# Two encoder layers on one core: normalised x of the experts split straight from x, modulation weights in units of one contraction tile

## The chip, the cores and the metric

The kernel runs on one core of a Trainium2 chip. The metric is the device time of one execution in microseconds (us), from a run without the profiler; below it is the median of three such runs. Two further numbers belong to one profiled execution: its own time, and its span, from its first instruction to its last.

## The reference

Two layers are computed on 256 tokens of width 1024. Each has a mixer half and an expert half, and each half scales and shifts its normalised input by a modulation that comes from a condition vector `c`:

```python
cond = silu(c)
for l in range(2):
    sh1, sc1, gt1, sh2, sc2, gt2 = split(cond @ w_ada[l] + b_ada[l], 6)   # w_ada[l]: 1024 x 6144
    h = rms_norm(x, g_norm1[l]) * (1 + sc1) + sh1
    x = x + gt1 * hybrid_mixer(h, ...)          # input projection, three attentions, gates, output projection
    h = rms_norm(x, g_norm2[l]) * (1 + sc2) + sh2
    x = x + gt2 * hier_moe(h, ...)              # router: best of 4 groups, best 2 of its 8 experts; SwiGLU
```

All arrays are float32. `cond @ w_ada` is a product of one row with a large matrix: 1024 rows are contracted, in eight tiles of 128 (the contraction tiles below).

## The kernel before

**Order.** The order of the instructions is written out by hand: what the program calls first stands first on its engine, and each engine works off its own list in order. A layer is a generator `mixer(l)` followed by `moe(l)`.

**Mixer.** `mixer` makes a list of 94 jobs: the input projection in 18 chunks of 384 columns (four jobs each), the two small projections of the latent attention, and the branch and output projections. A job has a first half, which splits a weight piece on ScalarE and VectorE into two rounded parts (lines 591 to 605), and a second half of matmuls on TensorE (607 to 622). The loop at lines 1380 to 1407 issues the first halves some four jobs ahead of the second halves, puts pieces of attention work between the jobs, and at chosen jobs one step of the modulation generator (`next(bg)`, 1406).

**Modulation.** `ada(l, g)` (386 to 421) computes one third of a layer's modulation row: g = 0 for the mixer's scale and shift, 1 for the experts', 2 for the two gates. A third has 2048 columns, in four blocks of 512. The condition vector's slice is the stationary operand, broadcast over 32 columns, so that block j goes to rows 32j to 32j+31 of one accumulator: four blocks use four separate 32-column groups of the array. A third's weights, 16384 columns of 128 rows, come contraction tile by contraction tile (2048 columns each), but are loaded in units of 3072 columns: five of 1.5 MB and one of 0.5 MB. A step takes one unit and issues its matmuls, six in each of the first five and two in the last; two more steps add the bias and transpose the row into columns. Layer 0's own first third is done by `ada_half` (423) in a layout of its own.

**Loads.** Weights come through the SP queue in one fixed order, `self.stream`, which `plan` (191) builds from `schedule` (152): the chunks in the order of their use, three jobs ahead, and the modulation units at the steps where they are due. `pump` (73) issues the next loads of that order while fewer than `self.ring` units are held, and is called whenever a buffer is given back. In the mixer `ring` is 3; the buffers are 12 of 1.5 MB (`u`), shared with the mixer's large intermediates. `early(l)` is 2 in layer 1: two modulation steps of its experts' third are done before the job loop, beside the normalisation of x (1307).

**Head of the experts.** `moe` (1412) transposes x into `x2T`, takes 1/rms from sums of squares that are there already, and writes the normalised x, `xn` (line 506, VectorE). TensorE computes the router's logits, `lg` (1426), and puts x into the result's accumulators, `y` (1431). ScalarE rounds xn to `xhi` (1441); GpSimd subtracts to get the rest, `xlo` (1442). VectorE picks groups and experts from the logits (1437 to 1486). TensorE sums the choices to ranks, `rk` (1488), then spreads the gate rows, `gth` (line 459, called at 1493). VectorE makes the positions `R` (1501) and the one-hot matrices `Poh` (1557), with which TensorE gathers the tokens, `ga` (1575); ScalarE copies them out as `xT` (1582), and the first expert's matmuls `A` start (1621). 32 experts follow, each with three 1.5 MB units, except that the third units of experts 0 and 1 come as 0.5 MB pieces (`load_pieces`).

Of the kernel before, what the change touches and what calls it, by code (L numbers as in the profile page):

```python
# [7 lines left out]
F32R = mybir.dt.float32r  # L8
BF = mybir.dt.bfloat16
I32 = mybir.dt.int32  # L10
AF = mybir.ActivationFunctionType
ALU = mybir.AluOpType
# [4 lines left out]
EPS = 1e-6  # L17
# [20 lines left out]
class Kern:  # L38
# [113 lines left out]
    def schedule(self, l):  # L152

        keys = []
        for c in range(10):
            keys += [('in', l, c)] * 4
            if c == 4:
                keys += [('uq', l)] * 4
            if c == 5:
                keys += [('ukv', l)] * 2  # L160
        first = len(keys)
        for c in range(10, 18):
            keys += [('in', l, c)] * 4
        last = len(keys)

        keys += [('bo', l, u) for u in [r // 3 for r in range(6)] + [2, 3, 3, 3] + [r // 3 for r in range(10, 18)]]
        if l == 0:
            keys[:12] = [keys[i] for i in self.FIRST]
        ada = [('ada', l, 1, u) for u in range(6)] + [('ada', l, 2, u) for u in range(6)]
        if l + 1 < self.layers:  # L170
            ada += [('ada', l + 1, 0, u) for u in range(6)]
        at = {}
        steps = []
        for k in ada:
            steps.append(k)
            if k[3] == 5:
                steps += [None, None]
        steps = steps[self.early(l):]
        lo, hi = 14 if l == 0 else 8, last - 5
        for n, k in enumerate(steps):  # L180
            at.setdefault(lo + n * (hi - lo) // len(steps), []).append(k)
        return keys, at
# [8 lines left out]
    def plan(self):  # L191
        a = self.a

        def src(k):
            if k[:3] == ('ada', 0, 0):
                c0 = k[3] // 3 * 8192 + k[3] % 3 * 3072
                return a['w_ada'][0, 0][:, c0:min(c0 + 3072, k[3] // 3 * 8192 + 8192)]
            if k[0] == 'ada':
                return a['w_ada'][k[1], k[2]][:, k[3] * 3072:min((k[3] + 1) * 3072, 16384)]
            if k[0] == 'in':  # L200
                return a['w_in'][k[1], k[2]]
            if k[0] in ('uq', 'ukv'):
                return a['w_' + k[0]][k[1]]
            if k[0] == 'bo':
                return a['w_bo'][k[1], k[2]]
            return a['w_e'][k[1], k[2]][:, k[3] * 3072:(k[3] + 1) * 3072]

        order = [('ada', 0, 0, u) for u in range(6)] + self.cut
        for l in range(self.layers):
            keys, at = self.schedule(l)  # L210
            seen = 0
            if l:
                order += [keys[0]] + [('ada', l, 1, u) for u in range(self.early(l))]
            for i in range(len(keys)):
                while seen < min(len(keys), i + 1 + self.AHEAD):
                    if keys[seen] not in order[-60:]:
                        order.append(keys[seen])
                    seen += 1
                order += [k for k in at.get(i, []) if k]
            order += [('e', l, e, u) for e in range(NE) for u in range(3) if ('e', l, e, u) not in self.beside(l)]  # L220
        s = [(k, src(k), 0) for k in order]
        first = [(k, x[:, i:i + 1536], i) for i in (0, 1536) for k, x, _ in s[6:9]]
        self.stream = deque(s[:3] + first[:3] + s[3:6] + first[3:] + s[9:])
        self.pieces = {}
# [161 lines left out]
    def ada(self, l, g):  # L386

        nc = self.nc
        ps = self.bank('ada')
        p = 0  # L390
        for u in range(6):
            key = ('ada', l, g, u)
            w = self.take(key)
            for i in range(6 if u < 5 else 2):
                kt, j = divmod(p, 4)
                self.mm(ps[32 * j:32 * j + 32], self.cond[:, kt:kt + 1].to_broadcast([128, 32]), w[:, i * 512:(i + 1) * 512], kt == 0, kt == 7)
                p += 1
            self.done(key)
            if u == 3:
                bz = self.load_bias(l, g)  # L400
            yield
        row = self.cp.tile([128, 512], F32, name=f"modrow_{l}", tag='modrow') if g == 2 else self.alloc('s', [128, 512], F32, 'modrow')
        nc.vector.tensor_add(row, ps, bz)
        self.free(ps, bz)
# [72 lines left out]
    def squares(self, ss, t, j, src=None):  # L477

        junk = self.alloc('s', [128, 512], F32, 'junk')
        self.nc.scalar.activation(junk, self.x[t][:, 512 * j:512 * j + 512] if src is None else src, AF.Square, scale=1.0 / 32,  # L480
                                  accum_out=ss[:, 2 * j + t:2 * j + t + 1])
        self.free(junk)

    def norm_x(self, name, ss=None, fill=None):

# [926 lines left out]
    def moe(self, l):  # L1412
        nc, tc = self.nc, self.tc
        ab = self.mod[l, 1]
        V = nc.vector
# [2 lines left out]
        self.router_row(l)  # L1418
        self.transposed(lambda t, k: self.x[t][:, 512 + k * 128:640 + k * 128], 4, None, None, full=xT[1:])
        self.router_row_all()  # L1420
        xn, rs = self.norm_x('xn2', self.ss)

        pt = self.bank('lg')
        for t in range(2):
            for kt in range(8):
                self.mm(pt[:, t * 64:t * 64 + 36], xT[kt // 4][:, kt % 4, t * 128:t * 128 + 128], self.wrs[:, kt], kt == 0, kt == 7)
        self.free(*xT)
        y = [[self.bank('y') for _ in range(2)] for _ in range(2)]
        for j in range(2):
            for t in range(2):  # L1430
                self.mm(y[t][j], self.ident, self.x[t][:, 512 * j:512 * j + 512], True, False)
        self.free(*self.x)
        xhi, xlo = ([self.alloc('w', [128, 1024], F32R, 'xp') for _ in range(2)] for _ in range(2))
        L = self.alloc('s', [128, 512], F32, 'L')
        lg = L[:, 0:72].rearrange("p (t n) -> p t n", t=2)
        for t in range(2):
            V.scalar_tensor_tensor(lg[:, t], pt[:, t * 64:t * 64 + 36], rs[:, t:t + 1], self.rrow,
                                   op0=ALU.mult, op1=ALU.add)
        self.free(pt)
        for t in range(2):  # L1440
            nc.scalar.activation(xhi[t], xn[t], AF.Copy)
            nc.gpsimd.tensor_sub(xlo[t], xn[t], xhi[t])
        self.free(*xn)
        self.load_pieces(l, 2)
        if l + 1 < self.layers:
            self.load_kr(l + 1)
            self.load_wr(l + 1)
# [42 lines left out]
        self.mm(pr[:, 32:64], self.tri[:, 0:128], Mb[:, 1], False, True)  # L1490
        self.mm(pr[:, 64:96], self.tri[:, 128:256], Mb[:, 0], True, False)
        self.mm(pr[:, 64:96], self.tri[:, 128:256], Mb[:, 1], False, True)
        gt = self.gate_halves(l)
        V.tensor_add(Mf, oh1, oh2)
        eg, gs, r2, sm = tmp(4), tmp(1), tmp(1), tmp(1)
        V.tensor_sub(eg, lgr, bc(gm, 4))
# [1 line left out]
        nc.scalar.activation(eg, eg, AF.Exp)  # L1498
        nc.scalar.activation(r2, r2, AF.Exp)
        nc.scalar.preload_act_table_set(SILU)  # L1500
        V.scalar_tensor_tensor(R, Mf, -4096.0, pr[:, 0:64].rearrange("p (t n) -> p t n", t=2), op0=ALU.mult, op1=ALU.add)

        def gates_and_blocks():
# [472 lines left out]
```

## Time and profile before

| | |
|---|---|
| median of three runs | 1390.2 us (1389.4 to 1391.21) |
| profiled execution, own time | 1390.37 us |
| its span | 1388.6 us |
| TensorE (PE) busy | 1329.2 us, 96% |
| VectorE (DVE), ScalarE (ACT), GpSimd (POOL) busy | 668.2, 538.4, 135.2 us |
| mean DMA rate over the span | 314 GB/s |
| mixer of layer 0, its experts | from the start to 347 us, to 715 us |
| mixer of layer 1, its experts | to 1017 us, to the end |

PE stands for matmuls and PEld for the loads of their stationary operand. A view in order of time gives start, duration, engine, line, operation, output and inputs, with the count of merged instructions (x12) and, in brackets, how long the engine had been idle before and what ended it. The matmul helper is line 102 for all callers, so the output's name tells which matmul it is.

### The profile page before, as it was taken

The numbers are of one execution on the slowest core, as the hardware profiler recorded it, in microseconds if no ns is written. First come the engines' busy times: TensorE is split into PE (matmuls) and PEld (weight loads), VectorE is DVE, ScalarE is ACT, GpSimd is POOL, SyncE is SP. The second block draws the span as 40 slices with busy tenths as digits, with TensorE's granted clock in tenths as the row PEclk, the third lists the DMA queues.
The fourth block names the chain that finished last, engine by engine and source line by source line (L and its number), as shares of the span: only waits on it lengthen the run. The fifth ranks groups of instructions, "written<-read, shape, count | busy, mean of one in ns | idle before, by whom it ended". The sixth has DMA issues, their size and how long they took to land. (4 is left out here: it accounts for less than half of the span.)

```text
span 1388.6 us, 19465 instructions
## 1 busy us (share of the span) xinstructions
PE 1329.2 (96%) x7666; PEld 869.3 (63%) x7666; DVE 668.2 (48%) x1417; ACT 538.4 (39%) x1140; POOL 135.2 (10%) x138
## 2 busy tenths in 40 slices
PE   5999999999899999999899999999999999999997
PEld 3788787887544444444358897888764444444443
DVE  5587564676623223332256775556762233323222
ACT  4554554574322222221155565447532222222211
POOL 0002064300100000000000202641010000000000
PEclk9999999999999999999999999999989999999999
DMA  9965457369589999999993626525858999999993
GB/s 373 374 246 222 184 204 289 129 246 360 222 345 425 425 425 424 425 426 425 420 421 151 227 91 232 191 94 202 358 214 318 404 425 425 425 424 427 424 424 147
DMA packets 45215, 437.95 MB, mean 315 GB/s; under 512 B 5080, under 2 KB 5608, under 8 KB 11328
## 3 DMA queue, kind: packets, MB, share of 16 engines
q1 hardware_dynamic: 44832, 435.78, 77.2%
q8 instruction: 62, 1.02, 0.3%
q0 software_dynamic: 288, 0.89, 0.2%
q14 instruction: 33, 0.27, 0.1%
HBM read 435.59 MB, written 1.05 MB: 314 GB/s over the span
## 5 line engine op out<-in xcount | busy, mean ns | idle before, releaser
L102 PE MATMUL in<-h,hH 128*128 128x384 f32 (+1 forms) x576 | 206.1, 358 | 3.7 <-ACT hH L1345 2.5
L1693 DVE TENSOR_TENSOR O<-O,gth 64x512 f32<-64x512 f32 (+1 forms) x132 | 88.8, 673 | 243.2 <-PE O L102 242.2
L102 PE MATMUL in<-h,hL 128*128 128x384 f32 (+1 forms) x576 | 195.3, 339 | 0.1
L102 PE MATMUL in<-l,hH 128*128 128x384 f32 (+1 forms) x576 | 194.5, 338 | 0.0
L1632 ACT ACTIVATE u<-A 64x384 f32<-64x384 f32 x64 | 31.1, 487 | 300.9 <-PE A L102 300.9
L102 PEld LDWEIGHTS in<-h,hH 128*128 128x128 f32 x576 | 109.0, 189 | 29.3 <-issue 17.1
L102 PEld LDWEIGHTS in<-h,hL 128*128 128x128 f32 x576 | 108.8, 189 | 1.4 <-DVE hL L1346 1.4
L102 PEld LDWEIGHTS in<-l,hH 128*128 128x128 f32 x576 | 109.2, 190 | 0.5
L1582 ACT ACTIVATE xT<-ga,modab 128x128 f32<-128x128 f32 x256 | 93.0, 468 | 20.6 <-PE ga L102 20.6
L1699 ACT ACTIVATE Op<-O 128x1024 fp32r<-128x1024 f32 x30 | 31.7, 1057 | 138.6 <-DVE O L1693 138.6
L1633 DVE SCALAR_TENSOR_TENSOR u<-A,m,u 64x384 f32<-64x384 f32 x64 | 39.4, 616 | 89.5 <-ACT u L1632 86.1
L102 PE MATMUL ga<-Poh,xp 128*128 128x256 f32 x512 | 71.4, 294 | 0.0
L102 PE MATMUL y<-Op,PTp 128*128 128x512 f32 x240 | 70.1, 415 | 0.0
L102 PEld LDWEIGHTS ga<-Poh,xp 128*128 128x128 f32 x512 | 65.8, 198 | 5.4 <-issue 4.0
L1602 DVE CAST PTp<-PTe 128x256 fp32r<-128x256 bf16 x32 | 13.6, 425 | 115.3 <-PE PTe L102 115.3
L803 POOL TENSOR_TENSOR rot<-TB,rope 128x256 f32<-128x256 f32 x8 | 11.7, 1487 | 488.6 <-ACT UC L873 429.3
L947 ACT ACTIVATE P<-P,m 128x256 f32<-128x256 f32 (+1 forms) x48 | 27.6, 576 | 79.2 <-DVE m L1005 37.1
L102 PEld LDWEIGHTS y<-Op,PTp 128*128 128x128 f32 x240 | 40.6, 188 | 21.0 <-issue 15.5
L1700 DVE TENSOR_TENSOR Op<-O,Op 128x1024 fp32r<-128x1024 f32 x30 | 36.8, 1225 | 33.8 <-ACT Op L1699 29.2
L1033 POOL TENSOR_SCALAR bias<-dist 128x128 f32<-128x128 f32 (+1 forms) x48 | 36.5, 761 | 5.2 <-PE oT L102 1.3
L1030 POOL TENSOR_SCALAR qz<-UC,gq 128x384 f32<-128x384 f32 x16 | 22.2, 1387 | 142.9 <-PE oT L102 72.7
L955 DVE TENSOR_SCALAR P<-P,m 128x256 f32<-128x256 f32 (+1 forms) x80 | 29.9, 407 | 1.8
(848 smaller groups left out, 2451.5 us busy)
## 6 DMA issues: line engine op xcount, KB each, us to landing
piece<-in_w_e SPq DMA_DIRECT2D x12, 512.0 KB, 6.8
w('ada', 0, 0, 0)_4_90<-in_w_ada SPq DMA_DIRECT2D x1, 1536.0 KB, 9.6
w('ada', 0, 0, 1)_5_92<-in_w_ada SPq DMA_DIRECT2D x1, 1536.0 KB
w('in', 0, 0)_9_104<-in_w_in SPq DMA_DIRECT2D x2, 768.0 KB, 16.5
w('in', 0, 1)_10_108<-in_w_in SPq DMA_DIRECT2D x2, 768.0 KB, 16.3
w('in', 0, 2)_11_110<-in_w_in SPq DMA_DIRECT2D x2, 768.0 KB, 12.2
w('ada', 0, 0, 3)_18_196<-in_w_ada SPq DMA_DIRECT2D x1, 1536.0 KB
w('ada', 0, 0, 4)_35_252<-in_w_ada SPq DMA_DIRECT2D x1, 1536.0 KB
```

The source lines that it names most:

```text
L102: self.nc.tensor.matmul(out, lhsT, rhs, start=start, stop=stop)
L947: nc.scalar.activation(dst, src, AF.Exp, bias=mx_neg[:, i:i + 1], scale=1.0, accum_out=sm[:, i:i + 1])
L955: nc.vector.tensor_scalar(dst, dst, r[:, i:i + 1], None, op0=ALU.mult)
L1030: nc.gpsimd.tensor_scalar(qz, M['qd'][:, pr::2, t * 128:t * 128 + 128], self.gq[:, l, 1 + hh:2 + hh], None, op0=ALU.mult)
L1033: nc.gpsimd.tensor_scalar(bias[:, lo:hi], self.dist[:, t, 256 + lo:256 + hi], -DIL_SLOPE[g][h], None, op0=ALU.mult)
L1582: nc.scalar.activation(dst, src, AF.Identity, scale=a2[:, kt:kt + 1], bias=s2[:, kt:kt + 1])
L1602: V.tensor_copy(PT[p], pv)
L1632: nc.scalar.activation(u[b:b + 64], A[c:c + 64, :384], AF.Silu)
L1633: V.scalar_tensor_tensor(u[b:b + 64], A[b:b + 64, :384], GC[e // 2][b:b + 64, e % 2:e % 2 + 1], u[b:b + 64], op0=ALU.mult, op1=ALU.mult)
L1693: V.tensor_mul(O[e // 2][b:b + 64, 512 * h + c:512 * h + c + n], o[c][p, :n], gt[p, c:c + n])
L1699: nc.scalar.activation(hi, whole, AF.Copy)
L1700: V.tensor_sub(lo, whole, hi)
```

## The change

Two parts. In the head of the experts, `xn` is no longer written: ScalarE makes `xhi` as the rounded x * (1/rms), with 1/rms as the per-row scale of its copy, and VectorE makes `xlo` as x * (1/rms) - xhi in one instruction. `low(0)` stands on VectorE ahead of the logits' first use, `low(1)` between the choice of the experts and the positions `R`. The gate rows (`gate_halves`) are issued right behind `y`, ahead of the ranks. The last two pieces are loaded after `low(1)`, and GpSimd's two loads for the next layer no longer stand behind its subtractions. In the modulation, a unit is one contraction tile: eight units of 2048 columns (1 MB) in place of six. A step takes two units and issues eight matmuls; a third has four such steps and two without weights. `early(l)` counts steps, so four units are taken early in layer 1, and the steps are spread anew over the same jobs.

```diff
-        for k in ada:
-            steps.append(k)
-            if k[3] == 5:
-                steps += [None, None]
+        for m, g in [(l, 1), (l, 2)] + [(l + 1, 0)] * (l + 1 < self.layers):
+            steps += [[('ada', m, g, u), ('ada', m, g, u + 1)] for u in range(0, 8, 2)] + [[], []]
         steps = steps[self.early(l):]
...
-                return a['w_ada'][k[1], k[2]][:, k[3] * 3072:min((k[3] + 1) * 3072, 16384)]
+                return a['w_ada'][k[1], k[2]][:, k[3] * 2048:(k[3] + 1) * 2048]
...
-        for u in range(6):
-            key = ('ada', l, g, u)
+        for kt in range(8):
+
+            key = ('ada', l, g, kt)
             w = self.take(key)
-            for i in range(6 if u < 5 else 2):
-                kt, j = divmod(p, 4)
-                self.mm(ps[32 * j:32 * j + 32], self.cond[:, kt:kt + 1].to_broadcast([128, 32]), w[:, i * 512:(i + 1) * 512], kt == 0, kt == 7)
-                p += 1
+            for j in range(4):
+                self.mm(ps[32 * j:32 * j + 32], self.cond[:, kt:kt + 1].to_broadcast([128, 32]), w[:, j * 512:(j + 1) * 512], kt == 0, kt == 7)
             self.done(key)
-            if u == 3:
+            if kt == 5:
                 bz = self.load_bias(l, g)
-            yield
+            if kt % 2:
+                yield
...
+    def norm_r(self, ss):
+        a = self.small(2)
+        self.nc.vector.scalar_tensor_tensor(a, ss[:, 0:2], EPS, ss[:, 2:4], op0=ALU.add, op1=ALU.add)
+        return self.rstd(a, 2)
...
-        xn, rs = self.norm_x('xn2', self.ss)
+        rs = self.norm_r(self.ss)
...
         self.free(*xT)
+
+        xhi, xlo = ([self.alloc('w', [128, 1024], F32R, 'xp') for _ in range(2)] for _ in range(2))
+        for t in range(2):
+            nc.scalar.activation(xhi[t], self.x[t], AF.Copy, scale=rs[:, t:t + 1])
+
+        def low(t):
+            V.scalar_tensor_tensor(xlo[t], self.x[t], rs[:, t:t + 1], xhi[t], op0=ALU.mult, op1=ALU.subtract)
+        low(0)
         y = [[self.bank('y') for _ in range(2)] for _ in range(2)]
         for j in range(2):
             for t in range(2):
                 self.mm(y[t][j], self.ident, self.x[t][:, 512 * j:512 * j + 512], True, False)
-        self.free(*self.x)
-        xhi, xlo = ([self.alloc('w', [128, 1024], F32R, 'xp') for _ in range(2)] for _ in range(2))
+        gt = self.gate_halves(l)
...
-        for t in range(2):
-            nc.scalar.activation(xhi[t], xn[t], AF.Copy)
-            nc.gpsimd.tensor_sub(xlo[t], xn[t], xhi[t])
-        self.free(*xn)
-        self.load_pieces(l, 2)
...
-        gt = self.gate_halves(l)
         V.tensor_add(Mf, oh1, oh2)
...
         nc.scalar.preload_act_table_set(SILU)
+        low(1)
+        self.free(*self.x)
+        self.load_pieces(l, 2)
         V.scalar_tensor_tensor(R, Mf, -4096.0, pr[:, 0:64].rearrange("p (t n) -> p t n", t=2), op0=ALU.mult, op1=ALU.add)
```

## Rows read from the trace of the kernel before

**Rows 1.** By stretch: length, busy PE PEld DVE ACT POOL, granted clock, DMA share, GB/s.

```profile
66.00:345.00 279.00, 276.54 (x1614) 226.03 (x1613) 185.39 (x388) 144.56 (x293) 61.51 (x62) 1.00 0.62 236
740.00:1015.00 275.00, 273.00 (x1584) 234.68 (x1583) 183.51 (x385) 149.83 (x311) 60.97 (x62) 1.00 0.51 197
...
365.00:369.00 4.00, 4.00 (x20) 3.63 (x20) 2.67 (x16) 3.68 (x9) 0.00 (x0) 0.56 0.02 6
```

**Rows 2.** Order of time, PE and PEld, around one modulation step of six matmuls.

```profile
740.06 0.33 PE L102 MATMUL in<-l,hH 128*128 128x384 f32 x1
...
740.24 0.34 PE L102 MATMUL in<-h,hL 128*128 128x384 f32 x1
...
740.50 1.91 PE L102 MATMUL ada<-ada', 1, 1, 2)_1137_5725,cond 128*32 128x512 f32 x12
740.96 0.12 PEld L102 LDWEIGHTS ada<-ada', 1, 1, 2)_1137_5725,cond 128*32 128x32 f32 x2 [0.30 <-issue]
741.39 0.12 PEld L102 LDWEIGHTS ada<-ada', 1, 1, 2)_1137_5725,cond 128*32 128x32 f32 x2 [0.31 <-issue]
...
742.35 0.44 PE L102 MATMUL in<-h,hH 128*128 128x384 f32 x1
```

**Rows 3.** Order of time, PE, around a third's last step, of two matmuls.

```profile
104.61 0.34 PE L102 MATMUL in<-h,hL 128*128 128x384 f32 x1
104.88 1.05 PE L102 MATMUL ada<-('ada', 0, 1, 5)_175_942,cond 128*32 128x512 f32 x4
105.86 0.33 PE L871 MATMUL trp<-pk,qn 128*128 128x128 f32 x1
```

**Rows 4.** Order of time, PE: what follows the early steps of layer 1.

```profile
717.77 2.16 PE L1313 MATMUL trx<-pk,xn 128*128 128x128 f32 x16 [0.16 <-DVE xn L506]
```

**Rows 5.** DMA issues of 100 to 260 us (columns: KB, us to landing).

```profile
'ada', 0, 2, 2)_244_1276<-in_w_ada SPq DMA_DIRECT2D x1, 1536.0 KB, 6.3
...
w('in', 0, 17)_548_2541<-in_w_in SPq DMA_DIRECT2D x1, 1536.0 KB, 11.8
...
'ada', 0, 2, 5)_325_1623<-in_w_ada SPq DMA_DIRECT2D x1, 512.0 KB, 5.6
```

**Rows 6.** Order of time, the experts' head in layer 0.

```profile
354.11 3.68 PE L102 MATMUL y<-x,pk 128*128 128x512 f32 x8
354.31 0.42 DVE L1437 SCALAR_TENSOR_TENSOR L<-lg,m,rrow 128x36 f32<-128x36 f32 x2 [0.66 <-PE lg L102]
354.43 4.65 POOL L1442 TENSOR_TENSOR xp<-xn,xp 128x1024 fp32r<-128x1024 f32 x2 [42.41 <-ACT xp L1441]
354.96 4.13 DVE L1464 SCALAR_TENSOR_TENSOR L<-L,rows 128x4 f32<-128x4 f32 x2
359.13 0.16 DVE L1465 TENSOR_REDUCE L<-L 128x2 f32<-128x8 f32 x1
...
363.26 1.98 PE L102 MATMUL gth<-modrow,pk 128*64 128x512 f32 x4
363.37 0.22 DVE L1501 SCALAR_TENSOR_TENSOR RT<-RT,rk 128x64 f32<-128x64 f32 x1 [0.20 <-PE rk L102]
...
365.17 3.64 PE L102 MATMUL ga<-Poh,xp 128*128 128x256 f32 x16
...
368.74 2.80 PE L102 MATMUL A<-w('e', 0, 0, 0)_659_3004,xT 128*64 128x384 f32 x16
```

**Rows 7.** Order of time, PE, two rows of the same head in layer 1.

```profile
1025.07 6.46 PE L102 MATMUL y<-x,pk 128*128 128x512 f32 x8
...
1038.16 2.80 PE L102 MATMUL A<-('e', 1, 0, 0)_1761_8443,xT 128*64 128x384 f32 x16
```

**Rows 8.** Groups by shape, DVE (columns: busy us, mean ns of one, idle before).

```profile
L1700 DVE TENSOR_TENSOR Op<-O,Op 128x1024 fp32r<-128x1024 f32 x30 | 36.8, 1225 | 33.8 <-ACT Op L1699 29.2 <-issue 2.4 <-ACTq L1798 2.2
...
L1464 DVE SCALAR_TENSOR_TENSOR L<-L,rows 128x32 f32<-128x32 f32 x8 | 1.7, 250 | 0.1
L495 DVE SCALAR_TENSOR_TENSOR junk<-x 128x512 f32<-128x512 f32 x2 | 1.3, 692 | 0.0
```

More of the change, by code (lines that the diff above doesn't have):

```diff
@@ L168, in schedule @@
             keys[:12] = [keys[i] for i in self.FIRST]
-        ada = [('ada', l, 1, u) for u in range(6)] + [('ada', l, 2, u) for u in range(6)]
-        if l + 1 < self.layers:
-            ada += [('ada', l + 1, 0, u) for u in range(6)]
         at = {}
         steps = []
-        for k in ada:
-            steps.append(k)
-            if k[3] == 5:
-                steps += [None, None]
+        for m, g in [(l, 1), (l, 2)] + [(l + 1, 0)] * (l + 1 < self.layers):
+            steps += [[('ada', m, g, u), ('ada', m, g, u + 1)] for u in range(0, 8, 2)] + [[], []]
         steps = steps[self.early(l):]
@@ L212, in plan @@
             if l:
-                order += [keys[0]] + [('ada', l, 1, u) for u in range(self.early(l))]
+                order += [keys[0]] + [('ada', l, 1, u) for u in range(2 * self.early(l))]
             for i in range(len(keys)):
@@ L218, in plan @@
                     seen += 1
-                order += [k for k in at.get(i, []) if k]
+                order += [k for step in at.get(i, []) for k in step]
             order += [('e', l, e, u) for e in range(NE) for u in range(3) if ('e', l, e, u) not in self.beside(l)]
@@ L389, in ada @@
         ps = self.bank('ada')
-        p = 0
-        for u in range(6):
-            key = ('ada', l, g, u)
+        for kt in range(8):
+            key = ('ada', l, g, kt)
             w = self.take(key)
-            for i in range(6 if u < 5 else 2):
-                kt, j = divmod(p, 4)
-                self.mm(ps[32 * j:32 * j + 32], self.cond[:, kt:kt + 1].to_broadcast([128, 32]), w[:, i * 512:(i + 1) * 512], kt == 0, kt == 7)
-                p += 1
+            for j in range(4):
+                self.mm(ps[32 * j:32 * j + 32], self.cond[:, kt:kt + 1].to_broadcast([128, 32]), w[:, j * 512:(j + 1) * 512], kt == 0, kt == 7)
             self.done(key)
-            if u == 3:
+            if kt == 5:
                 bz = self.load_bias(l, g)
-            yield
+            if kt % 2:
+                yield
         row = self.cp.tile([128, 512], F32, name=f"modrow_{l}", tag='modrow') if g == 2 else self.alloc('s', [128, 512], F32, 'modrow')
```

## The prediction

> **What bounds the kernel now.** I read the busy times by stretch first. In both mixers the matmul engine, PE, is busy for 276.5 of 279 us and 273 of 275 us at a granted clock of 1.00, while VectorE stands at 66 and 67%, ScalarE at 52 and 54% and the DMA engines at 62 and 51% [rows 1]. Whatever leaves PE there leaves the path; whatever is added to ScalarE, VectorE or the queues has room on average. Between mixer and experts it is otherwise: in 365 to 369 us PE is as good as busy, but at a mean clock of 0.56 and with DMA at 0.02 [rows 1]. There the order of time must be followed [rows 6]: TensorE ends y at 357.8 us and then waits, apart from five small matmuls, for VectorE's choice of experts, until 363.3. VectorE in turn is held by one line: two selections over four columns take 4.13 us (354.96), while the same line over 32 columns takes 0.25 each [rows 6, 8]. It is held exactly while GpSimd subtracts (354.43 to 359.08). The first A starts at 368.74.
>
> In the expert loop the first weight buffer comes free with A's first half, and until then no load is under way (DMA 0.02 [rows 1]). So an earlier A moves the stream of weights with it, and the loop's end too.
>
> **The modulation steps.** A step's price is what it puts between the matmuls around it. Six matmuls: 742.35 - 740.24 = 2.11 us, less the 0.17 at which matmuls of the mixer normally follow each other (740.06 to 740.24), is 1.94 us [rows 2]. Two matmuls: 105.86 - 104.61 = 1.25, less 0.17, is 1.08 us [rows 3]. What sets this is rounds, not matmuls. The four column blocks of one contraction tile use separate column groups, and each matmul is two passes; the step's later operand loads come in pairs, 0.43 us apart (740.96, 741.39) [rows 2], so a round with two of the four groups idle lasts as long as a full one. 1.94 is then four rounds of 0.43 and 0.22 around them, 1.08 is two rounds and the same 0.22.
>
> A third has cost 5 x 1.94 + 1.08 = 10.78 us. In the new cut a step is two whole tiles, again four rounds: 4 x 1.94 = 7.76 us, 3.02 less. Had I priced it by matmuls, the two steps give (1.94 - 1.08) / 4 = 0.215 us each, a step of eight costs 2.37 and a third 9.48, 1.30 less; that is the other end. I take rounds, because of the pairs' spacing.
>
> Four thirds run wholly inside the mixers (two of layer 0, layer 1's first, layer 1's last): 4 x 3.02 = 12.1 us. Layer 1's experts' third takes four units, not two, ahead of its jobs. There twelve matmuls were packed without a break, six rounds; now it is eight, 0.86 us more in front of the transposes, which had waited 0.16 us for xn [rows 4]; I charge 0.6. Inside the mixer three steps of 1.94 and one of 1.08 (6.90) become two (3.88): 3.02 less, net 2.4. Together 14.5 us off PE. Nothing in the mixer keeps PE waiting today beyond 2.5 and 2 us [rows 1], so most of it should come through; some of the steps hid latencies of VectorE and ScalarE that will now show. I take 1.5 us for that, between 0 and 6 (all of the 4.5 us of today's waits again, and a little).
>
> **The loads.** Bytes are the same. Following the load queue in the order of the program, a step's two units are asked for when the units of the step before are given back, three to four jobs earlier; a job is twelve matmuls at 0.17, 2.1 us, and attention work besides. A 0.5 MB load landed in 5.6 us, 1.5 MB in 6.3 to 11.8 [rows 5]; by these a 1 MB load lands in 6 us, two behind a chunk in about 12. Three jobs are 6.3 us bare and more with attention. It is close, and the chunks of the input projection that stand between the pairs are asked for one or two jobs ahead of their first split in some places. I price it at nothing, because the 12 buffers are handed out in turn and an older free one is usually there; uncovered, it is the second rival.
>
> **The experts' head, layer 0.** Removed: xn on VectorE, GpSimd's 4.65 us, and with it VectorE's hold: 4.13 becomes 2 x 0.25 or less, 3.6 us earlier [rows 6, 8]. Added: two ScalarE copies from x, which start as soon as 1/rms is there, as xn did, in place of the two from xn; `low(0)` and `low(1)`. The trace has no instruction of their form at this size; the subtraction of 128x1024 in line 1700 takes 1.23 us, and a scalar-tensor-tensor with two float32 inputs in SBUF takes 0.69 us for 512 columns, half of 1.23 and 0.08 more [rows 8]. I take 1.23 us each. `low(0)` stands where xn stood and ends about when the logits come, for which VectorE waited 0.66 us anyway [rows 6]: 0.2 us late. `low(1)` stands between the choice and R, where VectorE waited 0.20 us for the ranks: 1.0 us late. Balance at R: 3.6 - 0.2 - 1.0 = 2.4 us earlier. The gather ga has a second gain: it stood behind gth, at 365.17, 1.8 us after R; now gth is done beside VectorE's work, right after y, and ga follows the first one-hot, an estimated 0.75 us after R (R's 0.22, half of the 0.69 that 512 columns take [rows 8], and two hand-overs). So ga starts 2.4 + 1.0 = 3.4 us earlier. It took 3.64 us at the half level; where PE's break no longer lets the clock fall, half of that goes too. 3.4 to 5.2 us; I take 4.1, since the break between gate rows and gather stays at some 3 us and either level can be granted in it. The moved pieces are first used 15 us later, and DMA is idle then; GpSimd's two loads start earlier and nobody waits.
>
> The Trainium skill says otherwise of `low`: Vector Engine (DVE) Microarchitecture Reference, section 7, Points that are easy to get wrong, has a scalar-tensor-tensor with two SBUF sources that aren't bf16 run at half throughput. By it each would take about 2.3 us, and the two heads would give 4 us less in sum. Line 495 is such an instruction, with an accumulator besides, and its 692 ns don't show it [rows 8].
>
> The Trainium skill (TensorE: Matmul & The Clock Gate, What's actually happening) has the half rate as the state that an idle engine returns to and that activity lifts. By it a shorter break favours the upper end, 5.2.
>
> **Layer 1's head.** The same, but there the clock had already fallen ahead of y, which took 6.46 us where layer 0's took 3.68 [rows 6, 7]; y then ends at 1031.5, the gate rows behind it at 1032.5 to 1033.2, and the ranks can't start before that, where they did before. In that state only the gate rows ahead of ga are won, 0.6 us or a little more; at the full level it is layer 0's 3.4 to 5.2. I take 2.9. Both heads: 7.0, between 4 and 10.
>
> **The sum.** The profiled execution took 1390.37 us, 0.2 over the median; the sum is made against it. 14.5 - 1.5 + 7.0 = 20.0 us off: 1370.4, against the median 1370.2. I forecast 1370, with 1364 (14.5 + 10, and a little for the clock) to 1375 as its own range.
>
> **The rivals.** First, the heads pay little: TensorE's own y and gate rows at the half level become what ends last, in both layers, and `low(1)` is in the way. Then 13 + 3 = 16 us: 1374 to 1378. For it: layer 1's y. Against it: layer 0's y at full level. Second, late loads: at ten paired steps PE waits 1 to 1.5 us for the second unit, 10 to 15 us back: 1380 to 1385. For it: the reach of three jobs against two or three loads of 6 us; against: DMA at half load, and no wait of PE for a load in the mixers now. Third, matmuls and not rounds set a step's price: the modulation gives 4 x 1.30 + 0.4 = 5.6, the heads 7: 1377 to 1379. Against it stand the pairs 0.43 us apart. Fourth, on the other side: a chunk asked for one or two jobs ahead holds ScalarE, which works in order, with the attention's exponentials queued behind the split; PE waits for these. Some eight chunks are so placed, at the landing of 11.8 us [rows 5] against four jobs of 2.1: 3.4 us each, 27 us against the 20: 1397. It decides from landings of about 11 us at these places; 6.3 us is nearer to what single loads show. Fifth, that the mixers' time isn't PE's after all and nothing moves: 1388 to 1392; rows 1 leave little room for it.
>
> **How the numbers follow.** Forecast 0.65, heads pay little 0.12, late loads 0.10, price by matmuls 0.06, held ScalarE 0.05, nothing 0.02. Measurements of this kernel can tell about 0.2%, 2.8 us, from no change. Faster is all but the last two: 0.93; same 0.02; slower 0.05. The range from 1363 to 1381 takes in the forecast, the heads, the price by matmuls and the low edge of the late loads: somewhat over 0.8.
>
> **What would show it.** Modulation steps of 16 matmul records that put 1.94 us between their neighbours; PE as busy in the mixers as now, with the experts' first A of layer 0 some 12 us earlier than 368.7; line 1464 at 0.25 us; the `low` instruction at 1.2 us; ga right behind Poh. PE waits that end with a modulation load or a chunk's split would prove me wrong, as would a `low` of 2.3 us, or steps of 2.4 us.

## The result, and the profile after

The changed kernel took **1372.9 us** (median of four runs, 1371.5 to 1373.9) against 1389.95 for the kernel before beside it: a ratio of 0.9875, 95% interval 0.9858 to 0.9892, so 17.1 us off. The profiled execution had 1372.1 us, its span 1370.3. The forecast was 1370.

Where the 18.3 us between the two spans went, read from the starts of four matmuls in the order of time of both traces: the first transpose of a layer's normalised x (`trx`, which stands for the mixer's beginning), the first of the router's logits (`lg`), the first of the gather (`ga`) and the first `A` of the experts.

| stretch | before | after | difference |
|---|---|---|---|
| start to `trx`, layer 0 | 16.35 | 15.80 | -0.55 |
| mixer of layer 0, `trx` to `lg` | 334.16 | 331.13 | **-3.03** |
| head of layer 0, `lg` to `ga` | 14.66 | 11.07 | -3.59 |
| `ga` to `A` | 3.57 | 2.17 | -1.40 |
| experts of layer 0, `A` to `trx` | 349.03 | 347.94 | -1.09 |
| mixer of layer 1 | 303.12 | 296.91 | **-6.21** |
| head of layer 1, `lg` to `ga` | 14.03 | 12.87 | -1.16 |
| `ga` to `A` | 3.24 | 2.17 | -1.07 |
| experts of layer 1 to the end | 350.41 | 350.25 | -0.16 |

The heads gave 7.2 us. The mixer of layer 1, with two thirds of the modulation in it, gave the 6.0 that the forecast has for them and a little more. The mixer of layer 0, with three thirds, gave a third of its 9.1: this is the open question. Differences of whole layer-0 mixers are rough: the first part, ahead of every edited step (from `trx` to the thirty-first `in` matmul, the input projection's), took 16.3 to 17.9 us in the profiled executions, and 16.9 to 17.7 among the four kernels whose layer-0 mixer is that of the changed kernel. Where a microsecond matters, it is read at the place itself below.

**By stretch**, as [rows 1]:

```profile
66.00:345.00 279.00, 273.76 (x1644) 230.90 (x1642) 187.90 (x392) 146.49 (x299) 63.81 (x63) 0.99 0.63 244
112.00:116.00 4.00, 1.78 (x10) 1.65 (x10) 3.58 (x7) 3.62 (x7) 1.27 (x2) 0.94 0.74 316
116.00:120.00 4.00, 4.00 (x16) 4.00 (x16) 3.27 (x9) 1.58 (x4) 0.00 (x0) 0.50 0.00 0
...
740.00:1000.00 260.00, 258.00 (x1519) 226.54 (x1518) 177.74 (x368) 143.01 (x294) 60.62 (x62) 1.00 0.55 216
357.00:361.00 4.00, 3.13 (x27) 2.53 (x26) 3.51 (x20) 3.69 (x9) 0.00 (x0) 1.00 0.02 6
```

PE is now busy for 273.8 of 279 us in layer 0's mixer where it was 276.5. Of its 5.2 us of idle time 2.2 lie in one place, 112 to 116 us, and right behind it the granted clock is 0.50. Layer 1's mixer shows neither. In the last row the gather of layer 0 runs at 1.00, where [rows 1] had 0.56.

**What PE waits for** in layer 0's mixer, 66 to 345 us (total, times, longest):

```profile
PE in L102 <- DVE qn L791: 2.3, 1, 2.3
PE ada L102 <- DMA 'ada', 0, 2, 7)_317_1589<-in_w_ada: 1.4, 1, 1.4
```

The wait for `qn` was 1.0 before; the wait for the second unit of a modulation step is new. In order of time, before and then after, with the `in` matmul that starts the stretch and the one thirty further:

```profile
114.17 0.33 PE L102 MATMUL in<-h,hH 128*128 128x384 f32 x1
116.38 0.45 PE L102 MATMUL in<-h,hH 128*128 128x384 f32 x1 [0.99 <-DVE qn L792]
121.56 0.33 PE L102 MATMUL in<-h,hH 128*128 128x384 f32 x1
```

```profile
110.73 0.33 PE L102 MATMUL in<-h,hH 128*128 128x384 f32 x1
114.22 0.44 PE L102 MATMUL in<-h,hH 128*128 128x384 f32 x1 [2.26 <-DVE qn L791]
122.63 0.34 PE L102 MATMUL in<-h,hH 128*128 128x384 f32 x1
```

The same work takes 7.39 us before and 11.90 after: 4.5 more, of which 1.3 lie ahead of the matmul that waits and 3.2 behind it.

**A modulation step**, in order of time, as [rows 2, 3]:

```profile
744.89 0.34 PE L102 MATMUL in<-h,hL 128*128 128x384 f32 x1
...
745.16 1.07 PE L102 MATMUL ada<-ada', 1, 1, 6)_1169_5846,cond 128*32 128x512 f32 x8
...
746.05 1.04 PE L102 MATMUL ada<-ada', 1, 1, 7)_1221_6134,cond 128*32 128x512 f32 x8
...
747.02 0.77 PE L517 MATMUL tr<-pk,TA 128*128 128x128 f32 x5
```

747.02 - 744.89 = 2.13, less 0.17, is 1.96 us for eight matmuls, as for six before. The other steps cost 1.89 to 1.99 us by the same count, but for the one that waits for its unit (3.67).

**The early steps of layer 1**, as [rows 4]:

```profile
708.11 1.97 PE L1312 MATMUL trx<-pk,xn 128*128 128x128 f32 x16
```

The transposes no longer wait; they stand right behind the sixteen matmuls.

**The head of layer 0**, in order of time, as [rows 6, 8] (L1465 is the old 1464, L1504 the old 1501, and L1433 is `low`):

```profile
349.58 1.28 DVE L1433 SCALAR_TENSOR_TENSOR xp<-x,m,xp 128x1024 fp32r<-128x1024 f32 x1 [1.22 <-ACT xp L1430]
350.53 5.38 PE L102 MATMUL y<-x,pk 128*128 128x512 f32 x8
351.42 0.36 DVE L1465 SCALAR_TENSOR_TENSOR L<-L,rows 128x4 f32<-128x4 f32 x2
355.75 1.28 DVE L1433 SCALAR_TENSOR_TENSOR xp<-x,m,xp 128x1024 fp32r<-128x1024 f32 x1
355.83 1.08 PE L102 MATMUL gth<-modrow,pk 128*64 128x512 f32 x4
356.84 0.29 PE L102 MATMUL rk<-Mb,tri 128*128 128x32 bf16 x5
357.17 0.22 DVE L1504 SCALAR_TENSOR_TENSOR RT<-RT,rk 128x64 f32<-128x64 f32 x1
358.00 2.24 PE L102 MATMUL ga<-Poh,xp 128*128 128x256 f32 x16 [0.86 <-DVE Poh L1560]
```

The selections over four columns take 0.36 us in place of 4.13. `low` takes 1.28 us. `ga` starts 0.83 us after R, where it was 1.80. `y` is partly at the half level here (5.38 us in place of 3.68), and the ranks follow TensorE's gate rows, not VectorE's choice: VectorE has gone on to `low(1)` by 355.75.

**The head of layer 1**, as [rows 7]:

```profile
1010.67 4.93 PE L102 MATMUL y<-x,pk 128*128 128x512 f32 x8
1010.90 0.42 DVE L1443 SCALAR_TENSOR_TENSOR L<-lg,m,rrow 128x36 f32<-128x36 f32 x2 [1.95 <-PE lg L102]
...
1016.53 0.29 PE L102 MATMUL rk<-Mb,tri 128*128 128x32 bf16 x5
```

### The profile page after: what moved, and what is told of

It reads as the page before. It is cut to its first block, busy times and chain, and to the rows that moved or that the text cites. A ratio compares the mean times of both kernels' runs of the same rounds, so it can differ in the third digit from the quotient of the medians.

```text
span 1370.3 us, 19479 instructions
## 1 busy us (share of the span) xinstructions
PE 1314.2 (96%) x7666; PEld 869.8 (63%) x7666; DVE 662.4 (48%) x1413; ACT 537.8 (39%) x1140; POOL 127.3 (9%) x134
## 4 chain that ended last, share of the span: by engine, by line
PE 40%; DVE 4%; ACT 3%; DMA 3%; issue 1%; ACTq 0%; DVEq 0%; SPq 0%
PE A L102 12%; PE in L102 8%; PE O L102 6%; PE ga L102 2%; PE br L102 2%; DMA e', 1, 30, 0)_2189_10784<-in_w_e 2%; PE y L102 2%; PE out L102 1%; PE ada L102 1%; DMA e', 1, 31, 2)_2212_10907<-in_w_e 1%; PE S L102 1%; DVE u L1636 1%; ACT P L946 1%; PE oT L102 1%; DVE l L597 1%
## 6 DMA issues: line engine op xcount, KB each, us to landing
w('in', 0, 1)_10_108<-in_w_in SPq DMA_DIRECT2D x2, 768.0 KB, 18.2
```

## The experiments

Theory to begin with: the change's two parts add up, the head pays as forecast, and in layer 0's mixer a longer modulation step had hidden VectorE's lateness at `qn`. Rivals: the parts disturb one another; the fall of the clock, or the load, is the whole loss.

### One part at a time

`e_mod` is the kernel before with the hunks of `schedule`, `plan` and `ada` alone, `e_head` with those of `norm_r` and `moe` alone.

> The kernel before with the modulation's new cut alone; the experts' head is that of before. Theory A (the two parts add up, and the modulation gave what the comparison of the two traces leaves to it: 3.4 us up to the end of layer 0's mixer, 6.3 in layer 1's, 0.6 to 1 elsewhere): 10 to 11 us off, 1379 to 1380, ratio 0.992 to 0.993; PE's wait for qn near 112 us, some 2.3 us long, and its wait for the unit (0, 2, 7), 1.4 us, are there as in the changed kernel, and the clock falls behind the first of them. Rival B (the modulation gives the 13 us that I forecast and the two parts get in each other's way): 1377, ratio 0.9906, and the head alone then gives less than 5.

> The kernel before with the new head of the experts alone; the modulation is that of before. Theory A: the mixers of both layers take as long as before, to 0.5 us, and the two heads give 7 to 8 us: 1382 to 1383, ratio 0.9945 to 0.995. From the router's logits to the first A of the experts 13 us in layer 0 in place of 18.2, and 15 in place of 17.3 in layer 1. Rival B (the parts get in each other's way): under 5 us or over 9 us.

Measured: `e_mod` 1382.4 us, ratio 0.9942 (0.9924 to 0.9959), 7.9 off; `e_head` 1381.5, 0.9935 (0.9919 to 0.9952), 8.8 off. Sum 16.7, both together 17.1: they add up, within intervals of 2.4 us each way. Both medians lie outside what was expected, the modulation under its 10 to 11 us and the head over its 7 to 8; `e_mod`'s profiled execution has one more fall of the clock among layer 1's experts (352.1 us against 350.4). `e_mod`'s mixers take 331.09 and 296.94 us, those of the changed kernel, with the same two waits of 2.3 and 1.4 us; `e_head`'s take 334.03 and 303.05, those of before. `e_head`'s `lg` to `A` is 14.4 us in layer 0, not 13, since its gather ran at the half level; in layer 1 it is 13.2, not 15.

```profile
353.40 3.68 PE L102 MATMUL y<-x,pk 128*128 128x512 f32 x8
358.57 0.28 PE L102 MATMUL rk<-Mb,tri 128*128 128x32 bf16 x5 [0.48 <-DVE RT L1500]
359.82 0.21 DVE L1510 SCALAR_TENSOR_TENSOR RT<-RT,rk 128x64 f32<-128x64 f32 x1
360.64 3.64 PE L102 MATMUL ga<-Poh,xp 128*128 128x256 f32 x16 [1.79 <-DVE Poh L1566]
```

With `y` at the full level (3.68), PE waits 0.48 us for the choice, and R comes 1.25 us behind the ranks in place of 0.33: here `low(1)` stands in the way by about 0.9, as the prediction has it. Which of the two ends last thus goes with the clock that `y` is granted.

The modulation gave the smaller share, 7.9 of the 13 that I gave it; the loss is its own, in layer 0.

### What makes qn late: cover, or VectorE's own list

`e_cover` moves the fourth weight step of layer 0's first third, and its two steps without weights:

```diff
-            at.setdefault(lo + n * (hi - lo) // len(steps), []).append(k)
+            i = lo + n * (hi - lo) // len(steps)
+            at.setdefault({3: 29, 4: 31, 5: 33}.get(n, i) if l == 0 else i, []).append(k)
```

> The changed kernel, with three steps of layer 0's first third moved: the fourth step with weights from job 23 to job 29, right ahead of the job whose second bank waits for qn, the two steps without weights from 27 and 30 to 31 and 33. Theory A (the old cut's longer steps hid qn's latency; the pause that shows now also brings the fall of the clock behind it): PE's wait for qn shrinks from 2.3 us to 0.5 or less, the granted clock stays at 1.00 from 110 to 125 us, and the logits of layer 0 come 4 to 5 us earlier, near 342.5: about 1368.5 in all, 0.997 of the changed kernel. Rival B (the fall of the clock has nothing to do with the pause): the wait shrinks, the clock falls here or elsewhere in the mixer all the same, 1.5 to 2 us earlier. Rival C (the weights come too late or the pause moves to another place): no gain, within 1 us.

Measured: 1370.3 us, 0.9859 of before (0.9843 to 0.9875). The mixer of layer 0 took 329.41 us, 1.7 less, not 4 to 5. The wait hardly shrank, 1.90 us in place of 2.26:

```profile
115.70 0.45 PE L102 MATMUL in<-h,hH 128*128 128x384 f32 x1 [1.90 <-DVE qn L792]
```

PE came 1.85 us later to the place (113.46 against 111.61) and `qn` came 1.5 us later too; 1.0 of either is a longer way to the mixer (`trx` at 16.84 against 15.80). But the clock stayed up (1.00 over 112 to 120 us, where the changed kernel has 0.72). So this cover did not take the wait away: none of the three expectations holds. What holds `qn` stands on VectorE, in the order of time of the changed kernel (VectorE and GpSimd, with an earlier piece of the same line ahead):

```profile
84.16 1.15 DVE L370 TENSOR_TENSOR dist<-dd,masks 128x256 f32<-128x256 f32 x4
...
102.26 5.56 POOL L802 TENSOR_TENSOR rot<-TB,rope 128x256 f32<-128x256 f32 x4 [57.68 <-DVE TB L791]
104.85 1.49 DVE L597 TENSOR_TENSOR l<-w('in', 0, 6)_189_1014,h 128x768 fp32r<-128x768 f32 x1
106.27 3.34 DVE L370 TENSOR_TENSOR dist<-dd,masks 128x256 f32<-128x256 f32 x4
...
109.53 0.94 DVE L597 TENSOR_TENSOR l<-w('in', 0, 6)_189_1014,h 128x768 fp32r<-128x768 f32 x1
110.40 1.00 DVE L778 TENSOR_REDUCE m<-sq 128x6 f32<-128x384 f32 x2
...
113.60 1.02 DVE L791 TENSOR_TENSOR qn<-in,m 128x384 f32<-128x384 f32 x2
```

VectorE works without a break, and in front of the reduction that begins `qn`'s chain stand four maxima of the distance table: 3.34 us beside GpSimd's rotations and what follows them there, where the same four took 1.15 alone at 84.16. They stood there in the old kernel too (VectorE):

```profile
108.33 3.34 DVE L375 TENSOR_TENSOR dist<-dd,masks 128x256 f32<-128x256 f32 x4
115.77 1.02 DVE L792 TENSOR_TENSOR qn<-in,m 128x384 f32<-128x384 f32 x2
```

The change brought PE to the place 3.4 us earlier (110.73 against 114.17), and `qn` only 2.2. `e_dist` moves the maxima:

```diff
-                later(15 + 4 * n, lambda: next(dist, None))
+                later((15, 19, 23, 33)[n], lambda: next(dist, None))
```

> The changed kernel, with one piece of work of VectorE moved: the last of the four pieces that fill the distance table (four maxima, 3.34 us near 106 us of the changed kernel's trace) is issued at job 33 in place of job 27. Theory A (VectorE works without a break from 99.9 to 112 us and is what makes qn late; the old cut's longer steps held PE back for it): qn is ready some 3 us earlier, PE's wait of 2.3 us for it is gone, the clock stays at 1.00 to 125 us, and the logits of layer 0 come 4.5 to 5.5 us earlier, near 342: about 1368, 0.9965 of the changed kernel. Rival B (the fall of the clock is not tied to the wait): the wait goes, the clock falls all the same near 115 us: 2 to 2.5 us earlier. Rival C (VectorE is late at the next place too): the wait moves to a split or another bank behind 115 us, less than 1 us.

Measured: **1367.8 us** (1366.4 to 1369.2), 0.9845 of before (0.9831 to 0.9858). The mixer of layer 0 took 326.14 us, 5.0 less than in the changed kernel: theory A. `qn`'s wait is gone and no fall follows. Moved, the four maxima take 1.16 us (order of time, VectorE):

```profile
121.86 1.16 DVE L370 TENSOR_TENSOR dist<-dd,masks 128x256 f32<-128x256 f32 x4
```

PE is busy through the whole of the stretch, at the full level (as [rows 1]):

```profile
112.00:120.00 8.00, 8.00 (x50) 8.00 (x50) 7.26 (x14) 5.33 (x11) 2.46 (x4) 1.00 0.45 169
```

The stretch of thirty matmuls from above now takes 6.12 us in place of 11.90:

```profile
111.81 0.33 PE L102 MATMUL in<-h,hH 128*128 128x384 f32 x1
...
117.93 0.33 PE L102 MATMUL in<-h,hH 128*128 128x384 f32 x1
```

The piece is thus worth 5.8 us at its place: 2.4 up to the matmul that waited, and 3.4 behind it, where the changed kernel's matmuls follow each other by 0.32 us in place of 0.17. The whole mixer shows only 5.0, mostly since its first part took 1.0 us longer in this execution.

Is that piece worth as much in the old kernel? `e_dist_old` is the kernel before with the same edit.

> The kernel before, with the last piece of the distance table at job 33 in place of job 27, and nothing else. Theory A (the old cut's longer steps hid all but 1.0 us of VectorE's lateness, and no fall of the clock hung on the rest): PE's wait for qn of 1.0 us goes, the clock stays at 1.00 in layer 0's mixer as it did, and the logits come 1.0 us earlier, near 349.5: 1389, ratio 0.999, against 0.9965 for the same move in the changed kernel. Rival B (the piece cost the old kernel as much as the new one, hidden in other waits): 3 us or more.

Measured: the mixer of layer 0 took 332.64 us, 1.5 less (theory A: 1.0), and PE's wait of 1.0 us is gone; the stretch takes 6.12 us in place of 7.39, 1.3 less. The whole came out lower than expected, 1386.1 us (1384.1 to 1388.4), 0.9969 (0.9955 to 0.9983): in the profiled execution the head of layer 0 was 0.9 us shorter and its experts 1.6, without a change in either. The experts' part is a fall of the clock that this execution lacks (below). In the mixer itself the old kernel hid most of what the new one pays: 1.3 against 5.8.

### The late unit

`e_unit` moves the fourth weight step of layer 0's second third:

```diff
-            at.setdefault(lo + n * (hi - lo) // len(steps), []).append(k)
+            i = lo + n * (hi - lo) // len(steps)
+            at.setdefault({9: 45}.get(n, i) if l == 0 else i, []).append(k)
```

> The changed kernel, with the fourth step of layer 0's second third moved from job 43 to job 45, so that its second unit has two jobs more, 4 us, to land. Theory A (that load was late by itself): PE's wait of 1.4 us for this unit is gone and nothing takes its place; the logits of layer 0 come 1.2 to 1.5 us earlier, near 345.7. Rival B (the ring of three held loads is what is full, so the lateness moves on): a wait of a similar size for the next unit or a chunk, and less than 0.5 us earlier.

Measured: 1372.1 us, 0.9873 (0.9857 to 0.989). PE's wait is gone, and PE waits for no other load; but the mixer of layer 0 is only 0.7 us shorter (330.40), 1.0 if counted behind the mixer's first part. That lies between the two theories. From each start to the next, summed, the attention's `S` and `oT` matmuls of layer 0's mixer took 34.3 us in place of 33.3: part of what was won is waited for there. The likely source is ScalarE, which now waits 1.84 us for the next chunk, with the attention's copies queued behind its split:

```profile
179.65 0.84 ACT L597 ACTIVATE h<-w('in', 0, 11)_351_1724 128x768 fp32r<-128x768 f32 x1 [1.84 <-DMA w('in', 0, 11)_351_1724<-in_w_in]
```

So the lateness moved on in part, to a chunk, as rival B has it; the changed kernel has no such wait there.

### The head

`e_gth` issues the gate rows behind the ranks again; `e_rank` does that too and issues both low parts ahead of the choice:

```diff
-        gt = self.gate_halves(l)
         L = self.alloc('s', [128, 512], F32, 'L')
...
         self.mm(pr[:, 64:96], self.tri[:, 128:256], Mb[:, 1], False, True)
+        gt = self.gate_halves(l)
```

```diff
         low(0)
+        low(1)
...
-        low(1)
         self.free(*self.x)
```

`e_sub` is the kernel before with one word changed:

```diff
-            nc.gpsimd.tensor_sub(xlo[t], xn[t], xhi[t])
+            V.tensor_sub(xlo[t], xn[t], xhi[t])
```

> The changed kernel, with the gate rows issued behind the ranks again, as before. Theory A (what ends last ahead of the ranks is now TensorE with y and the gate rows, while VectorE's second low part holds R to about the same time): the ranks come 0.9 us earlier in both layers, R 0 to 0.2, the gather 0 to 0.3 later than in the changed kernel, and the time is that of the changed kernel to 0.5 us. Theory B (as I forecast, the gate rows ahead of the ranks are worth 1.0 us at the gather): the gather stands 1.0 us later behind R in layer 0, and 0.5 or more in layer 1.

> The changed kernel, with both low parts issued ahead of the choice of the experts, and the gate rows behind the ranks. Theory A (in layer 1 VectorE waits 1.95 us for the logits, which takes in the second low part, and the ranks then need only y; in layer 0 there is no such wait): from the logits to the first A 15.0 becomes 14.2 us in layer 1, and stays at 13.2 to 13.5 in layer 0, at the clock of the changed kernel. Rival B (the second low part costs nothing where it stands, since the ranks end last): layer 0 gets 1.0 to 1.3 us longer, and layer 1 stays.

| `lg` to `ga`, `ga` to `A` | layer 0 | layer 1 | whole |
|---|---|---|---|
| changed kernel | 11.07, 2.17 | 12.87, 2.17 | 1372.9 |
| `e_gth` | 10.83, 3.60 | 12.26, 2.17 | 1374.5 (one run) |
| `e_rank` | 11.18, 3.45 | 11.10, 2.73 | 1373.4 (one run) |

`e_gth`'s gather stands 0.2 and 0.6 us nearer to the logits, not farther. At the same clock, with `y` at the full level, layer 0 takes 10.83 us with the gate rows behind the ranks (`e_gth`) and 10.83 with them ahead (`e_head`): that order is worth nothing up to the gather. Behind it both kernels lose over a microsecond in layer 0, since their gather ran at the half level (3.66 and 3.52 us in place of 2.24). In layer 1 `e_rank`'s gather is at the full level, and yet `A` comes 0.56 us later behind it:

```profile
1012.57 3.68 PE L102 MATMUL y<-x,pk 128*128 128x512 f32 x8
...
1020.08 2.17 PE L102 MATMUL ga<-Poh,xp 128*128 128x256 f32 x16
1020.20 0.60 ACT L454 ACTIVATE gth<-gth 128x512 f32<-128x512 f32 x1 [7.56 <-PE gth L102]
...
1021.00 1.28 ACT L1501 ACT_TABLE_LOAD   x1
1022.29 1.86 ACT L1585 ACTIVATE xT<-ga,modab 128x128 f32<-128x128 f32 x5
...
1022.81 1.56 PE L102 MATMUL A<-('e', 1, 0, 0)_1769_8457,xT 128*64 128x384 f32 x8 [0.56 <-ACT xT L1585]
```

ScalarE copies the gate rows out and loads its next table just when it should copy `xT`; the copy stands first in that list. Issued ahead of the ranks, the gate rows are copied before; so that order can pay, at `A`. It needn't: in layer 1 of `e_gth`, where the gather stands later behind the gate rows, `A` follows by 2.17 all the same. `e_rank`'s shorter way to the gather in layer 1 is more than the order can give, since its `lg` and `y` ran at the full level, and those of the changed kernel didn't. Neither expectation for `e_rank` holds as it stands: from the logits to `A` layer 1 takes 13.8 us, less than theory A's 14.2, and layer 0 14.6, 1.4 longer, of which 1.3 lie behind the start of the gather at the half level and 0.1 ahead of it. Single runs, 1.6 and 0.5 us over the changed kernel's median, can't tell more.

> The kernel before, with the two subtractions of the low part moved from GpSimd to VectorE, at the same place in the program, and nothing else. Theory A (GpSimd's subtraction held VectorE's small selections): the two selections over four columns take 0.36 to 0.5 us in place of 4.13, VectorE has 2 x 1.23 us more to do, and from the logits to the first A 18.2 becomes 16.7 to 17.2 us in layer 0, with a like gain in layer 1: 2 to 3 us off in all. Rival B (they were slow for another reason, their form or a wait that the trace doesn't name): they stay at 4 us, and the head gets 2 us longer.

Measured: 1384.9 us (one run). VectorE, order of time:

```profile
353.98 2.35 DVE L1442 TENSOR_TENSOR xp<-xn,xp 128x1024 fp32r<-128x1024 f32 x2
...
356.44 0.36 DVE L1464 SCALAR_TENSOR_TENSOR L<-L,rows 128x4 f32<-128x4 f32 x2
```

0.36 in place of 4.13: GpSimd's subtraction was what held VectorE. `lg` to `ga` is 2.6 us shorter in layer 0 (12.08) and 1.1 in layer 1 (12.91), of the 3.8 and 3.0 that `e_head` has over before (10.83, 11.06): the larger part of the head's gain in layer 0 comes from this one line. From the logits to the first `A` layer 0 gained 3.4 us (14.8 in place of 18.2), where 1.0 to 1.5 were expected. R comes 1.7 us earlier behind `lg`, and the gate rows between R and the gather take 1.08 us at the full level, where they took 1.98 at the half [rows 6].

### The mends together

`e_both` has `e_dist`'s and `e_unit`'s edits, `e_both_rank` `e_rank`'s besides.

> The changed kernel with both mends: the last piece of the distance table at job 33, and the fourth weight step of layer 0's second third at job 45. Theory A (the two waits stand by themselves): neither is left, the modulation's records of layer 0 from the latent projection to the output projection take 14.8 us in place of 16.4, some of it given back at the scores (1 us with the step's move alone): 0.5 to 1.4 us under the kernel with the distance table's move alone, 1366.4 to 1367.3. Rival B (what is won ahead of an attention piece is waited for there): the same time as that kernel, 1367.8 to within 0.3.

> As the kernel with both mends, and in the experts' head both low parts ahead of the choice, the gate rows behind the ranks. Theory A (the order in the head decides only where TensorE's y ends last): layer 1's gather comes 0.6 to 1.7 us earlier behind the logits than the 12.8 us of the changed kernel, layer 0's stays at 11.1 to 11.2; the first A follows the gather by 2.2 us or by 3.5, as the clock is granted, which the order doesn't set: within 1.5 us of the kernel with both mends. Rival B (the gate rows ahead of the ranks keep TensorE at work and so keep its clock up at the gather): A 1.2 us later behind the gather in both layers, 1 to 2 us longer in all.

Measured: `e_both` **1365.3 us** (1364.9 to 1367.3), 0.9828 of before (0.9815 to 0.9842): 7.5 us under the changed kernel and 2.4 under `e_dist`, more than I expected. Layer 0's mixer is 324.26 us, 1.9 less than with the table's move alone; 1.2 of it lie in the mixer's first part, which neither edit touches, and 0.7 behind it, inside theory A's 0.5 to 1.4. No wait of PE over 0.7 us is left there (ScalarE's, for the same chunk as in `e_unit`, is 2.0).

`e_both_rank` took 1367.5 us (1364.4 to 1369.5), 0.9835 (0.9821 to 0.9849): not to be told apart from `e_both`. From its two gathers to `A` it takes 3.61 and 2.72 us, `e_both` 2.17 and 3.38. The gather ran at the half level in 3 of 12 heads with the gate rows ahead of the ranks, and in 7 of 14 with the ranks ahead. In the twelve, these are just the three whose `y` ran at the full level (3.68 us); in the nine whose `y` took 4.9 to 6.1 us the gather was at the full one. So with that order a head paid the half level at one of the two places, never at both. With the ranks ahead there is no such pattern, and whether the order is the cause is not shown.

## Why the prediction was right, and where not

**PE bounds the mixers: right.** With the two waits out of the way, the mixer of layer 0 is 9.9 us shorter than before; three thirds at 3.02 and the old wait of 1.0 make 10.1. Layer 1's: 6.2 against 6.0.

**Rounds set a step's price: right.** Eight matmuls 1.96 us, six 1.94; the other end of that step, 2.37, is out. In front of layer 1's transposes the early steps cost the 0.6 us more that I charged: with a fall of the clock in both, the experts of layer 0 take 349.03 us before and 349.65 in `e_mod` and `e_dist`.

**"1.5 us for latencies that show, between 0 and 6": this step failed in size.** In layer 0 it measured 5.9, with the late unit: 1.3 at `qn` (2.3 against 1.0), 3.2 for the half level behind it, and 1.4 for the unit; that is nearly all of the 6.0 that are missing. In layer 1 it was nothing. So the first `A` of layer 0 came 8.6 us earlier (360.17), not some 12. I had read the waits of before as small and spread; I had not looked at what stood in VectorE's list ahead of the one wait of 1.0 us. `e_dist` and `e_dist_old` show the content of that step: the same maxima held `qn` in the old kernel, and PE, with three microseconds more of modulation ahead of it, was nearly as late. The clock had no place in my sum for the mixers.

**Loads at nothing: nearly.** One of the eighteen paired steps of the job loops waited, 1.4 us; a wait for a modulation load was one of my signs of being wrong. The rival of late loads had its mechanism right for one place, not ten. The held ScalarE of the fourth rival is out in this kernel, where its longest wait for a chunk in layer 0's mixer is 0.5 us; `e_unit` shows it at one chunk (1.84).

**The heads, 7.0 us: right in sum, 7.2, with its parts off.** VectorE's hold is gone (3.8 for 3.6). `low` takes 1.28 for 1.23. By the page of the Trainium skill that I weighed (Vector Engine (DVE) Microarchitecture Reference, section 7, Points that are easy to get wrong) it would have been an estimated 2.3, and the trace disagrees. What the first rival describes did happen: `y` at the half level and the gate rows behind it end last in both layers (the ranks at 356.84 and 1016.53 follow them). In layer 0 it cost 0.2 us up to the gather (11.07 against `e_head`'s 10.83, with `y` at the full level), in layer 1, where `lg` was slow too, 1.8 (12.87 against 11.06); so the gather came 3.6 us nearer to the logits in layer 0 and only 1.2 in layer 1. Of "ga off the gate rows' way, 1.0" `e_gth` and `e_rank` show nothing at the gather and at most 0.56 at `A`, by way of ScalarE. The clock made up for it, by luck: the gather itself became 1.4 and 1.1 us shorter, since it ran at the full level. I had allowed for either level there, but not seen that it would go with a slow `y`.

**The sum, 20.0, came out 2.9 us high by the medians and 1.7 by the two spans**, though layer 0's mixer alone puts it 4.5 high (6.0 missing, 1.5 allowed for). Between the spans most of the rest is luck: 0.55 us ahead of the mixer, and 1.7 because the profiled execution of the changed kernel lacks a fall of the clock that the one of before has among the experts of layer 0:

```profile
688.00:694.00 6.00, 5.13 (x22) 2.11 (x24) 1.23 (x2) 0.77 (x1) 0.00 (x0) 0.72 1.04 419
688.87 4.50 PE L102 MATMUL A<-'e', 0, 30, 0)_1081_5341,xT 128*64 128x384 f32 x16 [2.63 <-DMA 'e', 0, 31, 2)_1104_5464<-in_w_e]
```

The same place of the loop in the changed kernel:

```profile
680.00:686.00 6.00, 5.73 (x37) 2.64 (x38) 1.29 (x3) 0.47 (x2) 0.00 (x0) 1.00 1.04 419
680.27 2.80 PE L102 MATMUL A<-'e', 0, 30, 0)_1085_5347,xT 128*64 128x384 f32 x16 [2.63 <-ACTq L1801]
```

PE stands idle for 2.63 us there in both, 320 us behind the first `A`, ahead of the last two experts; `overflow` and its branch on the count of overflowing blocks are issued at this point.

With the modulation's new cut, the experts of layer 0 take 349.65 us with the fall (`e_dist`) and 347.94 without (changed kernel): 1.7 us.

## What to carry to other kernels

Work taken off the engine that bounds a stretch pays only as far as the others are early there: before counting it, follow the list of the next engine in order at each wait that already shows, however short, and see what stands in front of the awaited instruction. GpSimd arithmetic beside VectorE arithmetic on SBUF was dear for VectorE here; two of the larger gains (the head's low parts, the distance table) came with moves out of its way. A pause that opens on TensorE is to be priced at more than its length, since the work behind it can run at the half level.

## What the runs showed of the hardware

**GpSimd holds VectorE.** Two selections over four columns took 4.13 us beside GpSimd's subtraction, to the end of it (359.09 and 359.08), and 0.36 without; four maxima 3.34 us beside its rotations and 1.15 alone; one split of 128x768 1.49 and 0.94. The Trainium skill (SBUF — State Buffer, Who interferes with whom) says that a VectorE instruction with two inputs in SBUF contends with a GpSimd instruction that reads SBUF, and that the later one is blocked. The numbers agree with it; I had used the hold in the head and not looked for it in the mixer.

**The clock fell behind a pause.** In the changed kernel, `e_mod`, `e_unit`, `e_gth` and `e_rank`, PE idles 2.2 to 2.3 us ahead of `qn` and the granted clock then falls to the lower level (1.2 of 2.4 GHz) within 2 us of its resuming; in the kernel before, `e_head`, `e_sub` (1.0 us of idling there) and in `e_dist`, `e_dist_old`, `e_both`, `e_both_rank` (none) it doesn't. `e_cover`, with 1.9 us, has no fall. `e_dist` shows that without the pause the fall is gone; why 1.9 us in `e_cover` were followed by none stays open.

**The same pause brings a fall in some executions and not in others.** In all thirteen profiled executions PE idles 2.63 us at the branch in each expert loop, 26 times in all. The clock falls within 1.5 us of its resuming in 15 of them, 8 of 13 in layer 0 and 7 of 13 in layer 1, and not in the other 11, without a change there. Apart from the kernel's very end only three other falls begin among the experts, all of them some 16 us behind the first `A`. A fall in the loop costs 1.7 us. Two or three of them are as much as the runs of one kernel differ by (1371.5 to 1373.9), and a change of some tenths of a microsecond in a head can't be seen against them. What decides whether a pause of 2 to 3 us is followed by a fall stays open, and so does whether the fall behind `qn`, there in five executions of five, would come in every run.
